# A second level of block multiplication for one of the seven products of gate/up

## The chip, the core and the metric

The kernel runs on one core of a Trainium2 chip. Five engines work side by side, each through its own list of instructions in order: PE (TensorE, matmuls; its weight loads are shown as PEld), DVE (VectorE, elementwise work on two tensors), ACT (ScalarE, activations and copies), POOL (GpSimd) and SP (SyncE, which here only issues DMAs). An engine that must wait for another waits at the instruction that needs it, and everything behind that instruction on the same engine waits as well. The metric is the time of one execution on the device in microseconds; lower is better.

## The reference

Two layers of an encoder trunk of width 1024 over 1040 tokens. Each layer has a mixer and then a SwiGLU feed-forward network with 2816 hidden units. The change lies in the feed-forward network alone:

```python
def swiglu(h, w_gate_up, w_down):
    gate, up = jnp.split(h @ w_gate_up.astype(h.dtype), 2, axis=-1)
    return (jax.nn.silu(gate) * up) @ w_down.astype(h.dtype)

for l in range(DEPTH):
    h = h + hybrid_mixer(rmsnorm(h, norm1_w[l]), ...)
    h = h + swiglu(rmsnorm(h, norm2_w[l]), w_gate_up[l], w_down[l])
```

Everything is float32. [...]

## The kernel before

**Gate/up.** The hidden units are cut into 22 tiles of 128 (FT = 22). For one tile f the weights are a 2 x 2 block matrix: A11 and A12 are the gate's weights for the first and the second half of the model width, A21 and A22 the up's; each block is 512 x 128, held as 4 pieces of 128 x 128. The tokens' x is a 2 x 2 block matrix too: model width by token half, each half 520 tokens in layer 0 (the 16 meta tokens included) and 512 in layer 1. The eight block products are made as seven, by Strassen's scheme in Winograd's form: A11·B11, A12·B21, S1·T1, S2·T2, S3·T3, S4·B22 and A22·T4, where S1 to S4 are sums of weight blocks and T1 to T4 sums of x blocks. The T's are made once a layer, the S's for each tile.

Of one tile, four DMAs on SP load the blocks; A21, A22 and the two sums' tiles come from a ring of five buffers (`ck2`). DVE makes the sums (lines 1373 to 1378). `w_op` splits a block: ACT writes the high part (line 1089), DVE the low part (line 1090); the pairs go round seven slots. `prod` issues a product's matmuls, three for each of the 4 k pieces (lines 1108 to 1110). In layer 0 a half of 520 columns does not go into one bank of PSUM, so each product runs as two groups of 260 columns (NJ = 2); in layer 1 it is one group of 512. Products that share a bank are added up by PE; DVE adds or ACT copies each out to `g` and `u` (lines 1391 to 1422). The seventh, p4, adds A22·T4 to the bank that holds S2·T2 + S3·T3 and the sum goes to u's first half:

```python
            def p4(j):
                prod(ps["b", j], W["A22"], T["T4"], j, False)
                tt(out=part(u, 0, j), in0=pin(ps["b", j]), in1=part(u, 0, j), op=ALU.add)
```

Behind the products DVE and ACT form silu(g·r)·u·r on whole rows of 1040 or 1024 columns (lines 1436 to 1439), a DMA stores the row to `ad`, and for the first 11 tiles DVE also writes a difference of its halves to `td`. The first four tiles (NE = 4) have A11·B11 and A12·B21 done ahead, under the end of the mixer, so five products are left there.

**Down.** The product with w_down follows the same seven-product scheme, in units of 3 x 128 hidden units by 128 outputs. Its sums of weights (S1, S2, S3, each in place of the last) are made by `s_sum`; `a_load` loads the 192 KB blocks for them. The first S1 sums are made inside gate/up by `s_under`: in the code, sum n stands behind tile n + 8, for n from 0 to 7 (S_UP = 8), with one buffer U of tag `c` (two buffers) for both loads. The rest are made under the units of down's first product.

**What sets the order.** The code is written product by product; a scheduler then orders each engine's list by priority (the order of the code) and by the times of its own model, with buffers taken when they are free. So an instruction stands in an engine's list where the scheduler found it ready, not where the code has it: the first S sums, written behind tile 8 and later, stand in DVE's list among the first tiles. The chip runs each list strictly in order.

Of the kernel before, what the change touches and what calls it, by code (L numbers as in the profile page):

```python
# [42 lines left out]
def trunk(ctx: ExitStack, tc: tile.TileContext, xT, w_in, w_ba, w_out, w_gu, w_dn,  # L43
# [267 lines left out]
    for l in range(DEPTH):  # L311
# [900 lines left out]
        S_UP = 8  # L1212
# [35 lines left out]
        def s_sum(which, n, room=None):  # L1248

            S = s_raw(n)  # L1250
            if which == "S1":
                r, o = room or (s_room(), s_room())
                tt(out=S, in0=a_load(r, 1, 0, n), in1=a_load(o, 1, 1, n), op=ALU.add)
            elif which == "S2":
                tt(out=S, in0=S, in1=a_load(s_room(), 0, 0, n), op=ALU.subtract)
            else:
                tt(out=S, in0=a_load(s_room(), 1, 1, n), in1=S, op=ALU.subtract)

        def s_under(f):

            n = f - 8
            if 0 <= n < S_UP:
                s_raw(n)
                if n == 0:
                    s_raw(6)
                    dw["U"] = c4k("U")
                s_sum("S1", n, (dw["U"][:, 0:384], dw["U"][:, 384:768]))
# [76 lines left out]
        def down_begins(p):  # L1344
# [10 lines left out]
            elif p is p1_[2]:  # L1355
                dw["T", 1] = flat("P1", F32R)
                w_unit(3)
                w_unit(4)
                t_pair(3)
        for f in range(FT):  # L1360
            A11, A12, A21, A22 = raw4("raw"), raw4("raw"), raw4("ck2"), raw4("ck2")
# [17 lines left out]
            for n, a in ([("S3", A21), ("A22", A22), ("S4", s2t)] if end else  # L1379
                         [("S4", s2t), ("S3", A21), ("A12", A12), ("A22", A22)]):  # L1380
                if f >= NE or n != "A12":
                    W[n] = w_op(a)
            g, u = early[f] if f < NE else (row((X[1], Y[1])[f % 2] + "f"), row(X[1], F32, 3))
# [27 lines left out]
            def p7(j):  # L1411
                prod(ps["b", j], W["S3"], T["T3"], j, False)
                tt(out=part(u, 1, j), in0=pin(ps["b", j]), in1=part(u, 1, j), op=ALU.add)

# [16 lines left out]
            else:  # L1431
                for j in range(NJ):
                    for p in (p1, p5, p3, p6, p7, p2, p4):
                        p(j)
            gv, uv, rv = g[:, o0:L], u[:, o0:L], ss[:, o0:L]
            tt(out=gv, in0=gv, in1=rv, op=ALU.mult)
            tt(out=uv, in0=uv, in1=rv, op=ALU.mult)
            act(out=gv, in_=gv, func=AF.Silu)
            tt(out=uv, in0=uv, in1=gv, op=ALU.mult)
            dma(ad[f][:, o0:L], uv)  # L1440
            if f < NP:
                tt(out=gv[:, 0:NB].rearrange("p (g e) -> p g e", g=2), in0=half(uv, 1), in1=half(uv, 0), op=ALU.subtract)
                dma(td[f], gv[:, 0:NB])
            s_under(f)


# [227 lines left out]
```

## Time and profile before

| | us |
|---|---|
| median of 3 runs | 2451.37 |
| lowest and highest run | 2449.09 and 2451.5 |
| the profiled execution | 2449.55 |
| its span, first to last instruction | 2447.5 |
| gate/up of layer 0, end of tile 4 to end of tile 20 | 684.5 to 1002.2 |
| gate/up of layer 1, end of tile 4 to end of tile 20 | 1893.0 to 2197.6 |

Ends of tiles are the ends of line 1436's multiplications. In rows of engines or windows, a number of us is the time in which the engine was busy, x the count of instructions. In rows of the timeline the first number is the start in us, the second the duration, and a bracket holds the idle time before and what ended it. Names of tiles are the buffers' tags: `a`, `b`, `a3`, `b3f` and so on are reused through the layers, `rw` is tag ck2, `whi` and `wlo` are weight slots, `pa`, `pb`, `pf`, `pacc` the PSUM banks. In rows with a bare name the number is left out.

### The profile page before, as it was taken

How to read it: one execution, taken by the hardware profiler on the slowest of the kernel's cores; microseconds unless marked ns; L12 is line 12 of the kernel's file. 1: busy time of each engine (PE TensorE's matmuls, PEld its weight loads, DVE VectorE, ACT ScalarE, POOL GpSimd, SP SyncE). 2: the span in 40 equal slices, each digit the busy share in tenths (PEclk: the TensorE clock that was granted, in tenths of full speed). 3: DMA queues.
4: the chain of work that ended last, by engine and by line, in shares of the span. 5: the costliest groups of instructions: out<-in, count | busy, mean ns of one | idle time of the engine just before them, and what ended most of it. 6: DMA issues, size and time to landing. Idle time of an engine off the chain costs nothing. (4 is left out here: it accounts for less than half of the span.)

```text
span 2447.5 us, 44866 instructions
## 1 busy us (share of the span) xinstructions
PE 2427.6 (99%) x17366; PEld 2234.8 (91%) x17366; DVE 1794.2 (73%) x3313; ACT 1026.3 (42%) x1918; POOL 183.6 (8%) x285
## 2 busy tenths in 40 slices
PE   9999999999999999999999999999999999999998
PEld 8989999999999999999999988998988888888887
DVE  6789355869877777797856883557798777768886
ACT  5744322435333333444546543224453333334464
POOL 0360000011000000000001400010110000000000
PEclk9999999999999999999999999999999999999999
DMA  3436165623432222665524551556334222228733
GB/s 134 164 112 145 66 213 159 216 86 105 158 119 95 84 79 79 213 219 166 161 80 145 156 126 62 176 170 228 121 115 153 99 95 82 83 96 274 234 103 129
DMA packets 256509, 336.32 MB, mean 137 GB/s; under 512 B 92021, under 2 KB 148793, under 8 KB 256297
## 3 DMA queue, kind: packets, MB, share of 16 engines
q1 hardware_dynamic: 208024, 299.37, 38.1%
q0 software_dynamic: 8448, 21.42, 2.8%
q10 hardware_dynamic: 39824, 12.68, 2.1%
q8 instruction: 136, 2.23, 0.4%
q14 instruction: 77, 0.62, 0.1%
HBM read 254.52 MB, written 78.86 MB: 136 GB/s over the span
## 5 line engine op out<-in xcount | busy, mean ns | idle before, releaser
L177 PE MATMUL pacc<-a,whi 128*128 128x346 f32 (+1 forms) x752 | 244.4, 328 | 4.0 <-DVE b L329 2.3
L179 PE MATMUL pacc<-a,wlo 128*128 128x346 f32 (+1 forms) x752 | 242.9, 325 | 0.1
L177 PE MATMUL pacc<-b,whi 128*128 128x342 f32 (+3 forms) x648 | 225.7, 349 | 0.0
L179 PE MATMUL pacc<-b,wlo 128*128 128x342 f32 (+3 forms) x648 | 223.4, 347 | 0.0
L178 PE MATMUL pacc<-a,whi 128*128 128x346 f32 (+1 forms) x646 | 211.2, 327 | 0.0
L178 PE MATMUL pacc<-b,whi 128*128 128x342 f32 (+3 forms) x559 | 192.8, 345 | 0.0
L132 ACT ACTIVATE whi<-raw 128x512 fp32r<-128x512 f32 x144 | 89.8, 628 | 243.6 <-PE pacc L178 177.4
L177 PEld LDWEIGHTS pacc<-a,whi 128*128 128x128 f32 x752 | 141.3, 189 | 9.9 <-issue 4.1
L133 DVE TENSOR_TENSOR wlo<-raw,whi 128x512 fp32r<-128x512 f32 x144 | 106.0, 739 | 56.0 <-ACT whi L132 55.0
L179 PEld LDWEIGHTS pacc<-a,wlo 128*128 128x128 f32 x752 | 141.8, 189 | 1.7 <-issue 0.8
L179 PEld LDWEIGHTS pacc<-b,wlo 128*128 128x128 f32 x648 | 122.4, 189 | 10.4 <-issue 1.7
L177 PEld LDWEIGHTS pacc<-b,whi 128*128 128x128 f32 x648 | 122.4, 189 | 8.5 <-issue 0.6
L178 PEld LDWEIGHTS pacc<-a,whi 128*128 128x128 f32 x646 | 122.1, 189 | 3.8 <-issue 2.3
L1089 ACT ACTIVATE whi<-rw 128x512 fp32r<-128x512 f32 x98 | 61.4, 631 | 137.7 <-DVE rw L1377 43.9
L178 PEld LDWEIGHTS pacc<-b,whi 128*128 128x128 f32 x559 | 105.8, 189 | 7.8 <-issue 1.3
L1089 ACT ACTIVATE b<-rw 128x512 fp32r<-128x512 f32 x65 | 40.6, 631 | 132.9 <-PE pacc L1109 39.6
L1089 ACT ACTIVATE a<-rw 128x512 fp32r<-128x512 f32 x65 | 40.8, 630 | 112.7 <-PE pacc L1109 78.5
L1090 DVE TENSOR_TENSOR wlo<-rw,whi 128x512 fp32r<-128x512 f32 x98 | 67.3, 688 | 5.6 <-ACT whi L1089 4.9
L329 DVE TENSOR_TENSOR b<-pacc,rstd 128x346 f32<-128x346 f32 (+1 forms) x63 | 32.3, 512 | 34.7 <-PE pacc L179 34.3
L1326 DVE TENSOR_TENSOR P<-b,P 128x520 fp32r<-128x520 f32 (+1 forms) x71 | 48.3, 695 | 10.4 <-ACT P L1325 10.3
L1544 PE MATMUL pacc<-P,a 128*128 128x260 f32 x196 | 55.4, 283 | 0.0
L1542 PE MATMUL pacc<-P,a 128*128 128x260 f32 x196 | 55.3, 282 | 0.0
(1043 smaller groups left out, 8011.9 us busy)
## 6 DMA issues: line engine op xcount, KB each, us to landing
raw<-in_w_in SPq DMA_DIRECT2D x112, 256.0 KB, 2.8
rw<-in_w_gu SPq DMA_DIRECT2D x96, 256.0 KB, 2.7
raw<-in_w_gu SPq DMA_DIRECT2D x96, 256.0 KB, 2.8
rec<-vkd SPq DMA_DIRECT2D x61, 256.0 KB, 2.9
b<-ad SPq DMA_DIRECT2D x55, 260.0 KB, 3.6
a<-ad SPq DMA_DIRECT2D x55, 256.0 KB, 3.8
rw<-in_w_dn SPq DMA_DIRECT2D x68, 192.0 KB, 3.6
ad<-a SPq DMA_DIRECT2D x21, 520.0 KB, 2.9
```

The lines of the kernel that those rows point to most:

```text
L132: lastw[0] = act(out=hi, in_=raw[:, 0:kk, :], func=AF.Copy)
L133: lastw[1] = tt(out=lo, in0=raw[:, 0:kk, :], in1=hi.bitcast(F32), op=ALU.subtract)
L177: mm(ps[:, :n], wh, xh[:, n0:n1], start=(k == 0), stop=False)
L178: mm(ps[:, :n], wh, xl[:, n0:n1], start=False, stop=False)
L179: mm(ps[:, :n], wl, xh[:, n0:n1], start=False, stop=(k == K - 1))
L329: tt(out=t[:, n0:n1], in0=ps, in1=rstd[:, n0:n1], op=ALU.mult)
L1089: act(out=hi, in_=src, func=AF.Copy)
L1090: tt(out=lo, in0=src, in1=hi.bitcast(F32), op=ALU.subtract)
L1326: tt(out=lo, in0=r, in1=hi.bitcast(F32), op=ALU.subtract)
L1542: mm(ps, wh[:, k, :], th[:, c0:c1], start=st and k == 0, stop=False, skip_group_check=True)
L1544: r = mm(ps, wl[:, k, :], th[:, c0:c1], start=False, stop=e, skip_group_check=True)
```

## The change

Tiles 4 to 19 go in eight pairs (f even, f odd). For a pair the product A22·T4 is itself a 2 x 2 block product: rows are the two tiles' A22, the inner dimension is cut in two halves of two k pieces, and the columns of T4 into two parts (260 or 256). `second_level` makes it by the same scheme with seven sub-products of two k pieces each, in three banks (pA, pC, pD); pA gets four of them one after the other and is added out to `u` after each. It loads both A22 once more, makes four sums of half blocks, and splits three and a half blocks (`wa`, `ws`, `wt`, `wz`) in place of two. S3·T3 is now added to both halves of u, since p4 no longer follows in its bank. u stays unfinished until the pair is done; every third g of these tiles moves to a buffer of tag `c`.

The x sums that the sub-products need are made once a layer by `quarters`, in four parts written behind tiles 1, 2, 3 and 4, into three rows that the first tiles' g leave and one buffer of tag `c`.

S_UP goes from 8 to 4, and `s_under` loads these four sums' blocks behind tile 19 and adds them behind tile 20.

On DVE, in the first tiles of layer 0: ahead, before the change, a piece from the end of tile 0's work; L1253 are S1 sums of down (`b_820` is the sum, `U` the loaded block), L1437 to L1442 finish a tile, L1090 are low parts of weights, L1406 and L1409 add products to g.

```order
L1442 TENSOR_TENSOR b_613_6137<-a_614_6138 128x520
L1374 TENSOR_TENSOR rw_6958<-rw_6957,raw_6949 128x512
L1422 TENSOR_TENSOR a_624_6211<-pf_6637,a_624_6211 128x260
L1253 TENSOR_TENSOR b_820_8275<-U_8277 128x384
L1406 TENSOR_TENSOR b_623_6210<-pb_6704,a_624_6211 128x260
L1090 TENSOR_TENSOR wlo_6803<-rw_6781,whi_6802 128x512
L1409 TENSOR_TENSOR b_623_6210<-pacc_6705,b_623_6210 128x260
L1406 TENSOR_TENSOR b_633_6283<-pb_6807,a_634_6284 128x260
L1436 TENSOR_TENSOR b_623_6210<-b_623_6210,rstd_5487 128x1040
L1409 TENSOR_TENSOR b_633_6283<-pa_6808,b_633_6283 128x260
L1406 TENSOR_TENSOR b_633_6283<-pf_6875,a_634_6284 128x260
L1253 TENSOR_TENSOR b_820_8275<-U_8277 128x384
```

After it, a piece that stands earlier on DVE, among the weights of tiles 0 and 1; L1378 to L1380 are the first x sums (`tr` their buffer, `a_649` is T4), L1452, L1453 and L1457 weight sums.

```order
L1090 TENSOR_TENSOR wlo_6455<-rw_6442,whi_6454 128x512
L1378 TENSOR_TENSOR tr_6778<-a_649_6417 128x520
L1379 TENSOR_TENSOR tr_6778<-a_649_6417 128x520
L1457 TENSOR_TENSOR rw_6609<-raw_6607,rw_6609 128x512
L1090 TENSOR_TENSOR wlo_6461<-rw_6436,whi_6460 128x512
L1453 TENSOR_TENSOR rw_6616<-rw_6615,raw_6607 128x512
L1090 TENSOR_TENSOR a_661_6449<-rw_6615,a_661_6449 128x512
L1380 TENSOR_TENSOR tr_6778<-tr_6778 128x520
L1489 TENSOR_TENSOR b_613_6137<-pacc_6465,a_614_6138 128x260
```

The S sums have left the first tiles, and the x sums stand there, the first of them before tile 0's first addition to g (L1489).

On DVE, in the middle of layer 0's gate/up: before, the end of one tile's second half. L1413 adds S3·T3 to u's second half and L1422 A22·T4 to its first, L1437 and L1439 finish u (`a_918`), the other rows belong to the next tiles.

```order
L1413 TENSOR_TENSOR a_918_9250<-pacc_9347,a_918_9250 128x260
L1090 TENSOR_TENSOR a_661_6449<-rw_9449,a_661_6449 128x512
L1395 TENSOR_TENSOR a_938_9482<-pb_9484,a_938_9482 128x260
L1374 TENSOR_TENSOR rw_9688<-rw_9687,raw_9679 128x512
L1422 TENSOR_TENSOR a_918_9250<-pacc_9347,a_918_9250 128x260
L1437 TENSOR_TENSOR a_918_9250<-a_918_9250,rstd_5487 128x1040
```

After, the end of a pair: L1420 are the additions from the second level's banks to the two u (`a_932`, `a_952`), L1496 and L1498 the two additions of S3·T3.

```order
L1420 TENSOR_TENSOR a_932_9100<-pf_9487,a_932_9100 128x260
L1090 TENSOR_TENSOR wlo_9564<-rw_9554,whi_9563 128x512
L1521 TENSOR_TENSOR b3f_9299<-b3f_9299,rstd_5487 128x1040
L1420 TENSOR_TENSOR a_932_9100<-pb_9489,a_932_9100 128x260
L1456 TENSOR_TENSOR rw_9554<-raw_9546,rw_9554 128x512
L1496 TENSOR_TENSOR a_952_9300<-pacc_9385,a_952_9300 128x260
L1498 TENSOR_TENSOR a_952_9300<-pacc_9385,a_952_9300 128x260
L1090 TENSOR_TENSOR a_661_6449<-rw_9554,a_661_6449 128x512
L1420 TENSOR_TENSOR a_932_9100<-pf_9487,a_932_9100 128x260
L1420 TENSOR_TENSOR a_952_9300<-pacc_9488,a_952_9300 128x260
```

One addition behind each tile's last product has become seven behind each pair, mixed with the next tile's weights and sums; bank pA is pf_9487 here.

The diff:

```diff
         td = dram.tile([NP, 128, NB], F32, name=nm("td"))
         dw = {}
         nr = [0, 0, 0]
-        S_UP = 8
+        S_UP = 4
 
         def flat(tag, dt=F32):
             return big(tag, dt).rearrange("p a b -> p (a b)")
...
                 return dw["X"][:, 384 * r:384 * r + 384]
             return dw["B"][:, 5 * NB + 384 * (r - 2):5 * NB + 384 * (r - 2) + 384]
 
-        def s_sum(which, n, room=None):
+        def s_sum(which, n):
 
             S = s_raw(n)
             if which == "S1":
-                r, o = room or (s_room(), s_room())
-                tt(out=S, in0=a_load(r, 1, 0, n), in1=a_load(o, 1, 1, n), op=ALU.add)
+                tt(out=S, in0=a_load(s_room(), 1, 0, n), in1=a_load(s_room(), 1, 1, n), op=ALU.add)
             elif which == "S2":
                 tt(out=S, in0=S, in1=a_load(s_room(), 0, 0, n), op=ALU.subtract)
             else:
...
 
         def s_under(f):
 
-            n = f - 8
-            if 0 <= n < S_UP:
-                s_raw(n)
-                if n == 0:
-                    s_raw(6)
-                    dw["U"] = c4k("U")
-                s_sum("S1", n, (dw["U"][:, 0:384], dw["U"][:, 384:768]))
+            for n in range(S_UP):
+                if f == FT - 3:
+                    if n % 2 == 0:
+                        dw["U", n // 2] = c4k("U")
+                    a_load(s_raw(n), 1, 0, n)
+                    dw["u", n] = a_load(dw["U", n // 2][:, 384 * (n % 2):384 * (n % 2) + 384], 1, 1, n)
+                elif f == FT - 2:
+                    tt(out=s_raw(n), in0=s_raw(n), in1=dw["u", n], op=ALU.add)
 
         def w_unit(u):
 
...
                 w_unit(3)
                 w_unit(4)
                 t_pair(3)
+        tq = {}
+
+        def quarters(n):
+
+            v = lambda t, k0, j: t[:, k0:k0 + 2, E * j:E * j + E].bitcast(F32)
+            hi, lo = T["T4"]
+            if n == 0:
+                two_rows = c4k("tr")
+                tq["raw"] = [two_rows[:, NB * q:NB * q + NB].rearrange("p (k e) -> p k e", k=2) for q in range(2)]
+            a, b = tq["raw"]
+
+            def split(i, r):
+                t = row(Y[1], F32R, 3) if i != 3 else sb.tile([128, L], F32R, tag="c", bufs=2, name=nm("tq"))
+                tq[i] = [t[:, NB * q:NB * q + NB].rearrange("p (k e) -> p k e", k=2) for q in range(2)]
+                act(out=tq[i][0], in_=r, func=AF.Copy)
+                tt(out=tq[i][1], in0=r, in1=tq[i][0].bitcast(F32), op=ALU.subtract)
+
+            if n == 0:
+                tt(out=a, in0=v(hi, 0, 1), in1=v(hi, 0, 0), op=ALU.subtract)
+                tt(out=b, in0=v(lo, 0, 1), in1=v(lo, 0, 0), op=ALU.subtract)
+                tt(out=a, in0=a, in1=b, op=ALU.add)
+                split(1, a)
+            elif n == 1:
+                tt(out=b, in0=v(hi, 2, 1), in1=a, op=ALU.subtract)
+                tt(out=b, in0=b, in1=v(lo, 2, 1), op=ALU.add)
+                split(2, b)
+            elif n == 2:
+                tt(out=a, in0=v(hi, 2, 0), in1=b, op=ALU.subtract)
+                tt(out=a, in0=a, in1=v(lo, 2, 0), op=ALU.add)
+                split(4, a)
+            else:
+                tt(out=b, in0=v(hi, 2, 1), in1=v(hi, 0, 1), op=ALU.subtract)
+                tt(out=a, in0=v(lo, 2, 1), in1=v(lo, 0, 1), op=ALU.subtract)
+                tt(out=b, in0=b, in1=a, op=ALU.add)
+                split(3, b)
+
+        def second_level(f, us):
+
+            Rf, Rg = raw4("ck2"), raw4("ck2")
+            dma(Rf, w_gu[l, f - 1, 1, :, 4:8, :])
+            dma(Rg, w_gu[l, f, 1, :, 4:8, :])
+            SA, SB = raw4("ck2"), raw4("ck2")
+            a, b = slice(0, 2), slice(2, 4)
+            tt(out=SA[:, a], in0=Rg[:, a], in1=Rg[:, b], op=ALU.add)
+            tt(out=SA[:, b], in0=SA[:, a], in1=Rf[:, a], op=ALU.subtract)
+            tt(out=SB[:, a], in0=Rf[:, a], in1=Rg[:, a], op=ALU.subtract)
+            tt(out=SB[:, b], in0=Rf[:, b], in1=SA[:, b], op=ALU.subtract)
+            wa, ws, wt, wz = w_op(Rf), w_op(SA), w_op(SB), w_op(Rg[:, b])
+            pick = lambda w, q: [t[:, q] for t in w]
+            bx = lambda k0, j: [t[:, k0:k0 + 2, E * j:E * j + E] for t in T["T4"]]
+            pA, pC, pD = pbank(), pbank(), pbank()
+
+            def sub(ps, w, t, first):
+                for k in range(2):
+                    mm(ps[:, :E], w[0][:, k, :], t[0][:, k, :], start=first and k == 0, stop=False, skip_group_check=True)
+                    mm(ps[:, :E], w[0][:, k, :], t[1][:, k, :], start=False, stop=False, skip_group_check=True)
+                    mm(ps[:, :E], w[1][:, k, :], t[0][:, k, :], start=False, stop=k == 1, skip_group_check=True)
+
+            def to(i, j, ps):
+                v = half(us[i][:, o0:L], 0)[:, j, :]
+                tt(out=v, in0=ps[:, :E], in1=v, op=ALU.add)
+
+            sub(pA, pick(wa, a), bx(0, 0), True)
+            to(0, 0, pA)
+            sub(pC, pick(ws, a), tq[1], True)
+            to(1, 1, pC)
+            sub(pD, pick(wa, b), bx(2, 0), True)
+            to(0, 0, pD)
+            sub(pA, pick(ws, b), tq[2], False)
+            to(0, 1, pA)
+            sub(pC, pick(wt, b), bx(2, 1), False)
+            to(0, 1, pC)
+            sub(pA, pick(wt, a), tq[3], False)
+            to(1, 1, pA)
+            sub(pA, wz, tq[4], False)
+            to(1, 0, pA)
+
+        waiting = []
         for f in range(FT):
+            two = NE <= f < FT - 2
             A11, A12, A21, A22 = raw4("raw"), raw4("raw"), raw4("ck2"), raw4("ck2")
             dma(A11, w_gu[l, f, 0, :, 0:4, :])
             dma(A21, w_gu[l, f, 1, :, 0:4, :])
...
             tt(out=A21, in0=A11, in1=A21, op=ALU.subtract)
             for n, a in ([("S3", A21), ("A22", A22), ("S4", s2t)] if end else
                          [("S4", s2t), ("S3", A21), ("A12", A12), ("A22", A22)]):
-                if f >= NE or n != "A12":
+                if (f >= NE or n != "A12") and not (two and n == "A22"):
                     W[n] = w_op(a)
-            g, u = early[f] if f < NE else (row((X[1], Y[1])[f % 2] + "f"), row(X[1], F32, 3))
+            if f < NE:
+                g, u = early[f]
+            else:
+                g = c4k("g") if two and f % 3 == 2 else row((X[1], Y[1])[(f % 3 if two else f) % 2] + "f")
+                u = row(X[1], F32, 3)
             ps = {}
 
 
...
             def p7(j):
                 prod(ps["b", j], W["S3"], T["T3"], j, False)
                 tt(out=part(u, 1, j), in0=pin(ps["b", j]), in1=part(u, 1, j), op=ALU.add)
+                if two:
+                    tt(out=part(u, 0, j), in0=pin(ps["b", j]), in1=part(u, 0, j), op=ALU.add)
 
             def p2(j):
                 if f >= NE:
...
                     down_begins(p)
             else:
                 for j in range(NJ):
-                    for p in (p1, p5, p3, p6, p7, p2, p4):
+                    for p in (p1, p5, p3, p6, p7, p2, p4)[:6 if two else 7]:
                         p(j)
-            gv, uv, rv = g[:, o0:L], u[:, o0:L], ss[:, o0:L]
+            gv, rv = g[:, o0:L], ss[:, o0:L]
             tt(out=gv, in0=gv, in1=rv, op=ALU.mult)
-            tt(out=uv, in0=uv, in1=rv, op=ALU.mult)
+            if not two:
+                tt(out=u[:, o0:L], in0=u[:, o0:L], in1=rv, op=ALU.mult)
             act(out=gv, in_=gv, func=AF.Silu)
-            tt(out=uv, in0=uv, in1=gv, op=ALU.mult)
-            dma(ad[f][:, o0:L], uv)
-            if f < NP:
-                tt(out=gv[:, 0:NB].rearrange("p (g e) -> p g e", g=2), in0=half(uv, 1), in1=half(uv, 0), op=ALU.subtract)
-                dma(td[f], gv[:, 0:NB])
+            waiting.append((f, g, u))
+            if f == NE:
+                quarters(3)
+            if two and f % 2 == 0:
+                continue
+            if two:
+                second_level(f, [w[2] for w in waiting])
+            for (n, g, u) in waiting:
+                gv, uv = g[:, o0:L], u[:, o0:L]
+                if two:
+                    tt(out=uv, in0=uv, in1=rv, op=ALU.mult)
+                tt(out=uv, in0=uv, in1=gv, op=ALU.mult)
+                dma(ad[n][:, o0:L], uv)
+                if n < NP:
+                    tt(out=gv[:, 0:NB].rearrange("p (g e) -> p g e", g=2), in0=half(uv, 1), in1=half(uv, 0), op=ALU.subtract)
+                    dma(td[n], gv[:, 0:NB])
+            waiting.clear()
             s_under(f)
+            if 0 < f < NE:
+                quarters(f - 1)
 
 
         hb = [big(X[0][0]), big(X[0][1])]
```

## The prediction

> **What bounds the kernel now.** I read the page's busy shares and chain first, then the windows by stage, then the waits and the timeline of the places that the change touches.
>
> ```profile
> PE 2427.6 (99%) x17366; PEld 2234.8 (91%) x17366; DVE 1794.2 (73%) x3313; ACT 1026.3 (42%) x1918; POOL 183.6 (8%) x285
> PE 40%; DVE 2%; DMA 1%; issue 1%; ACT 1%; ACTq 0%; SPq 0%; DVEq 0%; POOLq 0%
> ```
>
> PE is busy for 99% of 2447.5 us and alone carries the chain that ended last; fewer or shorter matmuls are the only thing that shortens the kernel, and any new wait of PE lengthens it. The profiled execution took 2449.55 us; the median of the three runs, 2451.37, is 1.8 above it.
>
> The windows by stage: gate/up of layer 0 (its first three tiles, then the tiles from 4 on), of layer 1 (the same two), and two pieces of layer 0's down stage.
>
> ```profile
> core 0: us, PE busy (x) PEld busy (x) DVE busy (x) ACT busy (x) POOL busy (x), PEclk, DMA share, GB/s
> 593.00:666.00 73.00, 71.47 (x590) 69.94 (x589) 65.47 (x111) 27.12 (x44) 0.00 (x0) 1.00 0.42 140
> 684.00:1008.00 324.00, 324.00 (x2705) 324.00 (x2705) 236.90 (x393) 108.80 (x196) 0.00 (x0) 1.00 0.26 88
> 1815.00:1863.00 48.00, 48.00 (x208) 38.53 (x206) 43.40 (x67) 18.18 (x27) 0.00 (x0) 1.00 0.44 140
> 1890.00:2198.00 308.00, 308.00 (x1333) 249.79 (x1332) 222.90 (x316) 100.64 (x159) 0.00 (x0) 1.00 0.27 92
> 1012.00:1048.00 36.00, 36.00 (x302) 36.00 (x301) 26.46 (x49) 16.21 (x31) 0.00 (x0) 1.00 1.03 360
> 1050.00:1090.00 40.00, 40.00 (x336) 40.00 (x336) 38.89 (x85) 18.57 (x37) 0.00 (x0) 1.00 0.67 206
> ```
>
> In the long part of gate/up PE never pauses and DVE has room (236.90 of 324 is 73%, 222.90 of 308 is 72%). In the first tiles DVE is at 90% in both layers (65.47 of 73, 43.40 of 48), and only in layer 0 does PE pause there, for 1.53 us. In the down stage the DMA engines are full for 36 us and then DVE is at 97%, yet PE does not wait.
>
> **What a matmul costs.** PE's records overlap, so the price is the distance of starts. First and last of 31 matmuls of 260 columns (layer 0), of 18 of 512 (layer 1), of 57 of 256 (the last stage):
>
> ```profile
> 800.29 0.28 PE L1108 MATMUL pacc<-P,a 128*128 128x260 f32 x1
> 803.90 0.28 PE L1108 MATMUL pf<-P,a 128*128 128x260 f32 x1
> ...
> 2100.03 0.39 PE L1108 MATMUL pb<-a,whi 128*128 128x512 f32 x1
> 2103.97 0.40 PE L1109 MATMUL pacc<-P,b 128*128 128x512 f32 x1
> ...
> 2421.79 0.28 PE L1544 MATMUL pacc<-P,wlo 128*128 128x256 f32 x1
> 2428.30 0.27 PE L1543 MATMUL pf<-P,b 128*128 128x256 f32 x1
> ```
>
> 3.61/30 = 0.1203 us, 3.94/17 = 0.2318 us, 6.51/56 = 0.1163 us.
>
> **The product A22·T4 (saved).** For a pair of tiles it was, in layer 0, 2 tiles x 2 halves x 4 k x 3 = 48 matmuls of 260 columns; now 7 sub-products x 2 k x 3 = 42. That is 6 x 0.1203 = 0.72 us a pair, 5.8 us over 8 pairs. In layer 1 it was 24 matmuls of 512 columns, 5.56 us; now 42 of 256, 4.88 us: 0.68 a pair, 5.4 us in all. Together 11.2 us, the whole of the gain.
>
> The layer-1 term rests on halving the columns halving the price. A weight load per matmul does not shrink: PEld is full in layer 0 (324.00 of 324) and 81% in layer 1 (249.79 of 308). The row of 256 columns settles it, 0.1163 against half of 0.2318, 0.1159. [...]
>
> **DVE per pair (added).** Starts of consecutive DVE instructions give its prices:
>
> ```profile
> 608.36 0.69 DVE L1090 TENSOR_TENSOR wlo<-rw,whi 128x512 fp32r<-128x512 f32 x1
> 608.96 0.69 DVE L1378 TENSOR_TENSOR rw<-raw,rw 128x512 f32<-128x512 f32 x1
> ...
> 650.05 0.42 DVE L1422 TENSOR_TENSOR a<-pa,a 128x260 f32<-128x260 f32 x1
> 650.39 0.42 DVE L1422 TENSOR_TENSOR a<-pacc,a 128x260 f32<-128x260 f32 x1
> ...
> 652.81 1.24 DVE L1437 TENSOR_TENSOR a<-a,rstd 128x1040 f32<-128x1040 f32 x1
> 653.96 0.70 DVE L1442 TENSOR_TENSOR b<-a 128x520 f32<-128x520 f32 x1
> 654.57 1.24 DVE L1439 TENSOR_TENSOR a<-a,b 128x1040 f32<-128x1040 f32 x1
> ```
>
> 0.60 us for 512 columns, 0.61 for 520, 0.34 for 260 (taken for 256 too), 1.15 for 1040. Per pair go two weight splits (1.2). Come three and a half splits (2.1 + one of 256 columns, 0.34), four weight sums of 256 columns (1.36) and seven additions out of the banks (2.38); the second addition behind S3·T3 replaces the one behind A22·T4. Net +5.0 us a pair. A pair's DVE time before is 0.73 x 40.4 = 29.5 us in layer 0 (2 x 168 matmuls x 0.1203 is 40.4) and 28.2 of 38.9 in layer 1; after, 34.5 of 39.7 and 33.2 of 38.3: 87%, between the 73% at which PE did not pause and the 90% at which it paused 1.53/73 = 2.1%. ACT gains 1.5 activations of about 0.6 us on a third of its time: nothing. Two more loads of 256 KB a pair go on DMA engines at 26%: nothing of themselves, but A21, A22 and four more tiles now pass through the same five buffers, 12 a pair instead of 8, so weights are ready later, and behind a load that waits on SP stand the next tile's loads.
>
> Bounds for PE's new waits over the 634 us behind the first tiles: 0, by the long windows, and 2.1% or 13.3 us, by the first tiles of layer 0. Layer 1's first tiles had no pause at 90%, so I stay near the lower end: 0.5% in layer 0 (1.7 us), 0.2% in layer 1 (0.6): 2.3 us.
>
> **The x sums in four parts (added); the S sums (moved).** 10 additions and 4 splits of 520 columns (512 in layer 1) at 0.61 us are 8.5 us of DVE a layer, in its fullest stretch. What leaves that stretch is large as well: the eight sums of down weights, written behind tiles 8 to 15, run in the first tiles, and DVE, which works in order, stands before them until their loads land.
>
> ```profile
> 617.46 0.69 DVE L1373 TENSOR_TENSOR rw<-rw,rw 128x512 f32<-128x512 f32 x1 [1.36 <-DMA rw<-in_w_gu]
> 635.10 0.56 DVE L1253 TENSOR_TENSOR b<-U 128x384 f32<-128x384 f32 x1 [1.37 <-DMA td<-b]
> 639.57 0.56 DVE L1253 TENSOR_TENSOR b<-U 128x384 f32<-128x384 f32 x1 [0.47 <-DMA U<-in_w_dn]
> 640.05 0.68 DVE L1090 TENSOR_TENSOR a<-rw,a 128x512 fp32r<-128x512 f32 x1
> ...
> L1253 DVE TENSOR_TENSOR b<-U x6: 547/555/559, 635.1 to 670.6; 128x384 f32<-128x384 f32 x6
>   DMA U<-in_w_dn: 5.2, 4
>   DMA td<-a: 1.8, 1
>   DMA td<-b: 1.4, 1
> ...
> PE pacc L1108 <- ACT whi L1089: 1.2, 2, 0.7
> PE pacc L1108 <- DVE b L1409: 0.2, 1, 0.2
> ...
> rw<-in_w_dn SPq DMA_DIRECT2D x68, 192.0 KB, 3.6
> ```
>
> Eight sums at 0.48 us (639.57 to 640.05) are 3.8 us a layer, and the 8.4 us of waiting in both layers is 4.2 each: 8.0 us leave, 8.5 come, so the stretch as a whole is no fuller. The places differ: the order sets the first five x additions, 3.0 us, among the splits for the first two tiles (from 609 us on), 20 us ahead of where the sums stood, and there PE already waits for splits and sums (the two rows of PE). The 1.36 us that DVE waits for a load at 617 takes part of it. So PE loses 3.0 − 1.4 = 1.6 us in layer 0. Layer 1 has the same five and no pause of PE there: I take 1.0. Bounds a layer: a gain of the 0.2 us at 641 that the first sums' wait precedes, and 8.5 us if all the new work came ahead of PE. Term: 2.6 us.
>
> **The S sums at their new places.** Four are loaded behind tile 19 into rows that the x parts held until tile 19's last sub-product; on SP, A22 and A12 of tile 21 stand behind two of these loads, with tile 20's products (168 x 0.1203 = 20 us) as cover: 0. If that cover is gone, it costs one load's landing, 3.6 us by the last row above, in each layer. The other four are summed in the down stage: 4 x 2 x 192 KB = 1.6 MB more at 360 GB/s is 4.4 us of DMA where the engines are full (1.03), and 1.9 us of DVE shortly before its 97%. The order puts most of these loads behind the first product's x loads, and PE had no wait at 97%, so I take 0.5 us a layer of a possible 0 to 4.4: 1.0 us.
>
> **The sum.** 11.2 − 2.3 − 2.6 − 1.0 = 5.3 us gained. Against the profiled execution 2444.3, against the median 2446.1; I say 2445.0, 0.26% under the median. What a measurement here can tell from no change is about 0.2%, 4.9 us, so the limits are 2446.5 and 2456.3.
>
> **Rivals.**
>
> *DVE delays PE a little in every pair, and the gain is gone.* Layer 0 at the first tiles' 2.1% over its 324 us pays 6.8 us instead of 1.7, layer 1 1.5 instead of 0.6: 6.0 less, net −0.7, 2450 to 2452, say 2451. For it: 87% is nearer to 90 than to 73, and weights that share five buffers come later. Against: DVE's room is spread over a pair of 39.7 us.
>
> *The bank of four sub-products becomes the bound: slower.* In second_level one bank, pA, gets four sub-products; after each, DVE must have added it out before the next one may write there, three times a pair. If DVE is in one of its 1.15 us instructions each time that counts once in a pair, PE stands 1.15 us a pair, 18.4 us over 16 pairs in place of 2.3: 2449.55 − 11.2 + 18.4 + 3.6 = 2460.4. It decides from (11.2 − 3.6)/16 = 0.48 us a pair on. For it: three sub-products are only 0.7 us long, less than one long DVE instruction. Against: in the pair of layer 0 whose additions are shown ahead, the order sets 28 to 36 other matmuls, 3.4 us and more, between two writes of pA.
>
> *A fixed price per matmul.* If 42 short ones with their weight loads cost more than 24 long ones (over 5.56/42 = 0.132 us each), layer 1 turns round; at 0.150 it loses 0.74 a pair, and the sum is 5.8 − 5.9 − 5.9 = −6.0: 2455.6. The 256-column rows stand against it; it keeps 0.03. [...]
>
> **How the numbers follow.** Forecast (faster) 0.50; gain eaten, within 0.2%, 0.27; bank pA 0.20; fixed price 0.03, near the upper limit, counted with slower. So faster 0.50, same 0.27, slower 0.23. The range runs from 2439.5 (all new waits near their lower ends: 2449.55 − 11.2 = 2438.4, a little above it) to 2457 (the second rival at 0.94 us a pair); above lies a little over 0.1, below under 0.1.
>
> **What the profile after would show.** PE: 96 matmuls more (48 fewer of 260 columns, 144 more that stand for halves of 512), 42 of them in lines of second_level per pair, their starts 0.12 apart; a pair of tiles from 4 on in 39.7 us in layer 0 and 38.3 in layer 1. DVE near 87% there. PE's waits in the first tiles of layer 0 grow from 1.5 to about 3 us, on splits of weights. No wait of DVE on loads of U in the first tiles. The forecast is wrong if PE's waits for DVE or ACT in gate/up behind the first tiles pass 3 us, if the pairs are longer than 39.9 and 38.5, or if the down stage begins with PE waiting for x or weights.

## The result and the profile after

The changed kernel takes 2458.12 us in the median (2455.67 to 2461.12), the kernel before 2450.32 beside it: a ratio of 1.0032, 95% interval 1.0024 to 1.0040. It is slower by 0.3%; the forecast was 2445.0, the range 2439.5 to 2457.0. The profiled execution of the changed kernel took 2461.12 us, its span 2459.1, so it is 3.0 above its median. Of the 11.6 us between the two spans 3.5 arose in the mixers (1.66 ahead of layer 0's gate/up, 1.82 between layer 0's down and layer 1's gate/up), which the change does not touch; the rest is in gate/up and down.

The page's busy shares and the engines' shares of the chain that ended last:

```profile
PE 2423.4 (99%) x17462; PEld 2236.4 (91%) x17462; DVE 1874.8 (76%) x3549; ACT 1047.2 (43%) x1958; POOL 184.3 (7%) x285
PE 38%; DVE 4%; DMA 2%; issue 1%; ACT 1%; SPq 0%; ACTq 0%; POOL 0%; DVEq 0%; POOLq 0%
```

PE has the 96 matmuls more that were forecast and is busy for 4.2 us less, yet the span is longer: the time is in PE's pauses. In the chain DVE has gone from 2% to 4%, DMA from 1% to 2%.

The same windows by stage as before, moved to where the stages now lie (first tiles and long part of layer 0, of layer 1, then the piece of layer 0's down stage in which DVE had been at 97%):

```profile
594.65:667.65 73.00, 69.98 (x572) 67.99 (x571) 67.85 (x116) 27.15 (x44) 0.00 (x0) 1.00 0.35 116
690.00:1012.00 322.00, 322.00 (x2688) 322.00 (x2687) 268.36 (x500) 117.94 (x216) 0.00 (x0) 1.00 0.32 105
1823.20:1871.20 48.00, 47.14 (x203) 37.54 (x202) 46.54 (x71) 18.27 (x28) 0.00 (x0) 1.00 0.35 111
1900.00:2208.00 308.00, 307.51 (x1490) 256.01 (x1489) 257.40 (x418) 109.23 (x177) 0.00 (x0) 1.00 0.32 106
1050.00:1090.00 40.00, 39.51 (x330) 39.29 (x329) 33.90 (x70) 18.69 (x37) 0.00 (x0) 1.00 0.71 219
```

In the long parts PE still does not pause, with DVE at 83% and 84%. The last row is the odd one: DVE, which had 38.89 us of work in these 40, now has 33.90, and it is not that there is less to do.

PE's longest pauses, from its timeline (start, duration, and in brackets the idle time before and what ended it):

```profile
614.39 0.39 PE L1110 MATMUL pacc<-b,a 128*128 128x260 f32 x1 [0.73 <-DVE a L1090]
616.88 0.39 PE L1110 MATMUL pf<-P,a 128*128 128x260 f32 x1 [0.54 <-DVE a L1090]
...
683.98 0.39 PE L1108 MATMUL pacc<-b,a 128*128 128x260 f32 x1 [1.59 <-DVE a L1478]
687.88 0.39 PE L1108 MATMUL pf<-P,whi 128*128 128x260 f32 x1 [2.20 <-ACT b3f L1503]
...
1091.76 0.36 PE L1642 MATMUL pf<-P,whi 128*128 128x260 f32 x1 [2.25 <-DVE a L1667]
...
2290.86 0.77 PE L1642 MATMUL pb<-P,whi 128*128 128x512 f32 x1 [3.65 <-DVE b L1667]
```

None of these was there before. Since PE's records overlap (a matmul of 260 columns is shown for 0.28 us, and the next starts 0.12 us behind it), the time lost is larger by the overlap: by the distance of starts the last four cost 1.76, 2.36, 2.41 and 3.81 us.

**Where the time went.** Lengths of stages from PE's starts; a stage ends with the first matmul of the next. "Down, P5" is down's second product, "down, rest" begins with the first matmul of its third, P3.

| us | before | after | difference |
|---|---|---|---|
| layer 0: first four tiles | 60.17 | 62.30 | +2.13 |
| tile 4 to the end of down's first product | 394.17 | 392.78 | −1.39 |
| down, P5 | 31.61 | 34.03 | +2.42 |
| down, rest | 157.97 | 159.54 | +1.57 |
| layer 1: first four tiles | 55.91 | 56.99 | +1.08 |
| tile 4 to the end of down's first product | 380.63 | 377.67 | −2.96 |
| down, P5 | 30.63 | 34.42 | +3.79 |
| down, rest | 155.64 | 157.11 | +1.47 |
| sum | 1266.73 | 1274.84 | +8.11 |

The 8.1 us agree with the 7.8 us between the medians. 9.25 us of loss are in down, whose own matmuls the change does not touch.

**The stop in down.** P3 goes on in the banks of P5, so its first matmul must wait until DVE has added P5's sums out of them (L1667). DVE's waits for loads between 1000 and 1092 us, and rows of its timeline (L1252 are S1 sums, L1254 S2 sums):

```profile
DVE b L1252 <- DMA b3f<-in_w_dn: 2.6, 3, 1.2
DVE b L1252 <- DMA b<-in_w_dn: 1.4, 2, 0.9
...
DVE b L1254 <- DMA b<-in_w_dn: 1.1, 1, 1.1
...
DVE b L1254 <- DMA b3f<-in_w_dn: 0.6, 1, 0.6
DVE S L1252 <- DMA b3f<-in_w_dn: 0.5, 1, 0.5
```

```profile
1070.57 0.42 DVE L1252 TENSOR_TENSOR b<-b3f,b 128x256 f32<-128x256 f32 x1 [0.90 <-DMA b<-in_w_dn]
...
1072.48 0.43 DVE L1252 TENSOR_TENSOR b<-b,b3f 128x256 f32<-128x256 f32 x1 [1.15 <-DMA b3f<-in_w_dn]
1073.53 0.56 DVE L1254 TENSOR_TENSOR b<-b,b3f 128x384 f32<-128x384 f32 x1 [0.62 <-DMA b3f<-in_w_dn]
...
1077.01 0.56 DVE L1254 TENSOR_TENSOR b<-b,b 128x384 f32<-128x384 f32 x1 [1.14 <-DMA b<-in_w_dn]
...
1091.18 0.43 DVE L1667 TENSOR_TENSOR a<-pf,a 128x260 f32<-128x260 f32 x1
```

DVE stands for 6.2 us before sums whose blocks have not landed; the same view of the kernel before lists no wait for a load there in layer 0. Its waits for other things are no longer than before, 12.1 us against 15.0. In layer 1 the waits for loads are 5.7 us, against 1.6 before. The rooms into which the blocks go (two in row `b3f`, two in `b`) are few, and the next load into one starts only when DVE has used the last: between 1000 and 1092 us SP, which issues these loads, waits 10.4 us for L1252 and L1254. From 1077 on DVE is busy without a gap (14.17 of 14.18 us) and never catches up: the addition that PE waits for stands at 1091.18 behind some 14 us of other work.

**The stop at tile 4.** ACT's row, then DVE's:

```profile
687.45 0.39 ACT L1503 ACTIVATE b3f<-pf 128x260 f32<-128x260 f32 x1 [2.96 <-DMA td<-b3f]
```

```profile
679.86 1.24 DVE L1536 TENSOR_TENSOR c<-c,b3f 128x1040 f32<-128x1040 f32 x1
...
682.88 0.70 DVE L1539 TENSOR_TENSOR b3f<-c 128x520 f32<-128x520 f32 x1
683.50 0.42 DVE L1478 TENSOR_TENSOR a<-pacc,a 128x260 f32<-128x260 f32 x1
...
687.45 0.43 DVE L1489 TENSOR_TENSOR b3f<-pacc,a 128x260 f32<-128x260 f32 x1 [2.22 <-DMA td<-b3f]
```

Tile 3's g has always been in `b3f`. The diff's new rule for g's row, f % 3 in place of f % 2, gives tile 4 this same row; before, it took the other one. Tile 3 must be finished and its difference stored from `b3f` to `td` before tile 4's first copy may be written there. DVE's last work on tile 3 (L1536, L1539) therefore stands ahead of an addition that frees a bank (L1478, first pause), and ACT and DVE then both wait for the store (second pause).

### The profile page after: what moved, and what is told of

Its sections match the earlier page's. It is cut to its first block, busy times and chain, and to the rows that moved or that the text cites. A ratio compares the mean times of both kernels' runs of the same rounds, so it can differ in the third digit from the quotient of the medians.

```text
span 2459.1 us, 45475 instructions
## 1 busy us (share of the span) xinstructions
PE 2423.4 (99%) x17462; PEld 2236.4 (91%) x17462; DVE 1874.8 (76%) x3549; ACT 1047.2 (43%) x1958; POOL 184.3 (7%) x285
## 5 line engine op out<-in xcount | busy, mean ns | idle before, releaser
L179 PEld LDWEIGHTS pacc<-b,wlo 128*128 128x128 f32 x648 | 122.8, 190 | 10.4 <-issue 1.7
L1089 ACT ACTIVATE whi<-rw 128x512 fp32r<-128x512 f32 (+1 forms) x120 | 73.4, 615 | 136.8 <-PE pf L1109 30.6
L1090 DVE TENSOR_TENSOR wlo<-rw,whi 128x512 fp32r<-128x512 f32 (+1 forms) x120 | 80.2, 670 | 5.4 <-ACT whi L1089 4.7
L1089 ACT ACTIVATE b<-rw 128x512 fp32r<-128x512 f32 (+1 forms) x70 | 42.7, 616 | 72.4 <-PE pacc L1109 26.6
L1089 ACT ACTIVATE a<-rw 128x512 fp32r<-128x512 f32 (+1 forms) x70 | 42.6, 616 | 61.1 <-PE pacc L1109 16.2
L1326 DVE TENSOR_TENSOR P<-a,P 128x512 fp32r<-128x512 f32 (+1 forms) x71 | 48.0, 692 | 11.3 <-ACT P L1325 11.3
L1644 PE MATMUL pacc<-P,a 128*128 128x260 f32 x196 | 55.4, 283 | 0.0
```

The lines of the kernel that those rows point to most:

```text
L179: mm(ps[:, :n], wl, xh[:, n0:n1], start=False, stop=(k == K - 1))
L1089: act(out=hi, in_=src, func=AF.Copy)
L1090: tt(out=lo, in0=src, in1=hi.bitcast(F32), op=ALU.subtract)
L1326: tt(out=lo, in0=r, in1=hi.bitcast(F32), op=ALU.subtract)
L1644: r = mm(ps, wl[:, k, :], th[:, c0:c1], start=False, stop=e, skip_group_check=True)
```

## Experiments

All times are medians; the ratios are to the kernel before, run beside each, with 95% intervals. Line numbers are each kernel's own. The expectations speak of a stop "behind down's first product": by the products' order in the trace it stands at the start of the third. The intervals of experiments 2, 3 and 7 include 1: by their times these kernels cannot be told from the kernel before, and what they show is read against the changed kernel and from the stages.

**1. The S sums alone.** The kernel before with one number changed.

```diff
-        S_UP = 8
+        S_UP = 4
```

> The kernel before with S_UP = 4 and nothing else: sums 4 to 7 of down weights are left to the down stage, as in the changed kernel, without the second level and the x sums in parts. Theory (the four extra sums in down are what stops PE behind down's first product): PE waits 2 to 4 us for DVE's additions at the start of the second product in each layer, runs 1.6 us at a lower clock behind that, and the time is 2450.3 + 2.4 + 3.8 + 2 x 1.6 = about 2459.7 (2456 to 2461). Rival (the stop comes from the second level, which brings tile 21 and its rows later): no wait there, 2449 to 2452.

Measured: 2461.12 us, 1.0047 (1.0032 to 1.0062). PE's rows:

```profile
1091.08 0.36 PE L1542 MATMUL pf<-P,whi 128*128 128x260 f32 x1 [1.71 <-DVE a L1567]
...
2290.53 0.76 PE L1542 MATMUL pb<-P,whi 128*128 128x512 f32 x1 [4.22 <-DVE b L1567]
```

The stop needs no second level. Four sums left to down make the kernel before as slow as the changed one, and the time is 0.1 above the range that was expected. P5 grows by 1.88 and 4.36 us, the rest by 0.10 and 1.50, together 7.8; another 1.3 us are lost in gate/up. PE's waits in layer 0's first tiles grow from 1.4 to 1.8 us, so there the S sums' leaving by itself gave nothing.

**2. Other rows for g.** The three buffers in another turn.

```diff
-                g = c4k("g") if two and f % 3 == 2 else row((X[1], Y[1])[(f % 3 if two else f) % 2] + "f")
+                g = c4k("g") if two and f % 3 == 0 else row((X[1], Y[1])[(f % 3 - 1 if two else f + 1) % 2] + "f")
```

> The changed kernel with g's three buffers taken in another turn, so that tile 4 takes the row that stands free and not the one that tile 3 has just left. Theory (the 4.1 us of PE at tiles 4 and 5 of layer 0, 0.8 in layer 1, come from ACT and DVE waiting for tile 3's rows to be stored): these waits go, 2458.1 - 4.9 = 2453.2. Rival (DVE at 87% is late there, whatever rows are used): the waits stay, 2457 to 2459. The last g also leaves the row in which down's weight sums are loaded one tile earlier: if that matters, another 1 to 3 us.

Measured: 2447.24 us, 0.9992 (0.9982 to 1.0001): 10.9 less than the changed kernel, more than expected. On DVE, tile 4's first additions to g now stand early, in row `a3f`, without a wait for a store; in layer 1 PE still stops in down:

```profile
672.29 0.43 DVE L1489 TENSOR_TENSOR a3f<-pacc,a 128x260 f32<-128x260 f32 x1 [0.68 <-PE pacc L1110]
...
683.39 0.42 DVE L1489 TENSOR_TENSOR a3f<-pf,a 128x260 f32<-128x260 f32 x1
...
2278.42 0.47 PE L1642 MATMUL pb<-P,whi 128*128 128x512 f32 x1 [3.15 <-DVE b L1667]
```

Layer 0 from tile 4 to the end of down's first product takes 388.55 us, 4.23 less than in the changed kernel, and PE has no pause there. The stop in layer 0's down has gone as well. The edit does two things, since the last tile's g also leaves the row in which S blocks are loaded; experiment 8 parts them.

**3. All eight S sums early again.** In the changed kernel, behind tiles 19 and 20.

```diff
-        S_UP = 4
+        S_UP = 8
...
-            for n in range(S_UP):
-                if f == FT - 3:
-                    if n % 2 == 0:
-                        dw["U", n // 2] = c4k("U")
-                    a_load(s_raw(n), 1, 0, n)
-                    dw["u", n] = a_load(dw["U", n // 2][:, 384 * (n % 2):384 * (n % 2) + 384], 1, 1, n)
-                elif f == FT - 2:
-                    tt(out=s_raw(n), in0=s_raw(n), in1=dw["u", n], op=ALU.add)
+            if f == FT - 3:
+                for n in range(S_UP):
+                    a_load(s_raw(n), 1, 0, n)
+                U = c4k("U")
+                for n in range(2):
+                    dw["u", n] = a_load(U[:, 384 * n:384 * n + 384], 1, 1, n)
+            elif f == FT - 2:
+                for n in range(S_UP):
+                    o = dw["u", n] if n < 2 else a_load(raw4("ck2").rearrange("p a b -> p (a b)"), 1, 1, n)
+                    tt(out=s_raw(n), in0=s_raw(n), in1=o, op=ALU.add)
```

> The changed kernel with all eight early sums of down weights made behind tiles 19 and 20 again (four more than it makes there). Theory: the stop behind down's first product goes, with the lower clock behind it: 2458.1 - 9.4 = 2448.7, if tiles 20 and 21 take the eight loads and four sums without waiting. Rival (the stop has another cause): 2457 to 2459, with PE still waiting 2 to 4 us at the start of the second product.

Measured: 2448.19 us, 0.9993 (0.9984 to 1.0003). P5 and the rest of down are back at the lengths before in both layers (31.61 and 157.98, 30.62 and 155.64). Tiles 20 and 21 take the loads and sums without a pause of PE. The pauses at tile 4 of layer 0 stay, 1.76 and 2.03 us.

**4. Both edits.**

> Both edits of the two kernels ahead in one. Theory (two separate losses, which add): 2458.1 - 4.9 - 9.4 = 2443.8, faster than before by 6.5 us, which is the saved matmuls less the first tiles' waits. Rival (the second level's work on DVE finds another place to be late, so that a removed wait comes back elsewhere): 2448 or more.

Measured: 2443.49 us, 0.9977 (0.9967 to 0.9986). The gains do not add: 10.9 and 9.9 would make 20.8, it is 14.6, because experiment 2 alone had already won back 3.8 us in layer 0's down and 1.9 in layer 1's, which experiment 3 wins back as well: 5.7 of the 6.2. The stages sum to 643.92 − 3.46 = 640.46 in layer 0 and 622.81 − 2.55 = 620.26 in layer 1: 6.0 us below the kernel before, where the theory said 6.5.

**5. The x sums tied to later places.** In the kernel of both edits.

```diff
-        def quarters(n):
+        def quarters(n, prev=None):
...
-                tt(out=a, in0=v(hi, 0, 1), in1=v(hi, 0, 0), op=ALU.subtract)
+                after(tt(out=a, in0=v(hi, 0, 1), in1=v(hi, 0, 0), op=ALU.subtract), prev)
...
-            tt(out=gv, in0=gv, in1=rv, op=ALU.mult)
+            g_done = tt(out=gv, in0=gv, in1=rv, op=ALU.mult)
...
-                quarters(f - 1)
+                quarters(f - 1, g_done)
```

(and `after` in the same way around the first instruction of each further part.)

> The kernel of both edits (2443.5), with the x sums in parts tied behind the finished g of tiles 1, 2 and 3, so that the first of them no longer stands among the weights of tiles 0 and 1. Theory (PE's new waits in the first tiles, 2.1 us in layer 0 and 1.1 in layer 1, come from the places of these sums on DVE, not from their number): the waits of 0.9 and 0.7 us near the start of layer 0's first tiles and of 0.7 us in layer 1 go, 2441 to 2442. Rival (DVE is full in the first tiles, so the same time is lost later in them): 2443 to 2445, with PE waiting at tiles 2 to 5.

Measured: 2441.18 us, 0.9961 (0.9946 to 0.9976), the fastest of all. The first tiles of layer 0 in the kernel of both edits, then in this one (same window, counted from the stage's start):

```profile
594.40:667.40 73.00, 69.92 (x571) 67.92 (x570) 67.79 (x115) 27.09 (x44) 0.00 (x0) 1.00 0.35 115
```

```profile
594.11:667.11 73.00, 71.20 (x588) 69.61 (x586) 66.46 (x113) 26.96 (x44) 0.00 (x0) 1.00 0.37 117
```

PE's pauses are down to 1.80 us (before the change 1.53), and the stage takes the 60.17 us that it took before; layer 1's takes 55.80. The work on DVE is nearly the same (91% of the window against 93%), so it was the places. In layer 1 the first tiles gain 0.77 us and the stretch behind them loses 1.19 (378.67 against 377.48). The intervals of experiments 4 and 5 overlap; the stage shows the difference, not the medians.

**6. The second level in layer 0 alone.** In the kernel of both edits, with the turn of g's rows in layer 1 as before the change.

```diff
-            two = NE <= f < FT - 2
+            two = l == 0 and NE <= f < FT - 2
...
-            if f == NE:
+            if l == 0 and f == NE:
                 quarters(3)
...
-            if 0 < f < NE:
+            if l == 0 and 0 < f < NE:
                 quarters(f - 1)
```

> The kernel of both edits (2443.5), with the second level and the x sums in parts in layer 0 alone; layer 1 keeps its product A22 times T4 of 512 columns. It measures what 42 matmuls of 256 columns save against 24 of 512. Theory (118.1 ns against 231.9 in the trace: 0.6 us a pair, 4.8 in all, less 0.8 to 1.1 in the first tiles): 2443.5 + 3.8 = about 2447.3. Rival (the shorter matmuls and their DVE work give layer 1 nothing): 2443 to 2444.

Measured: 2446.64 us, 0.9983 (0.9974 to 0.9993). Layer 1's stages sum to 622.73, the length before the change (622.81), against 620.26 with the second level: it is worth 2.5 us in layer 1 (3.15 by the medians, whose intervals overlap), less than the 3.8 expected.

**7. Fewer loads in down, the same additions.** In the changed kernel, for sums 4 to 7.

```diff
-                tt(out=S, in0=a_load(s_room(), 1, 0, n), in1=a_load(s_room(), 1, 1, n), op=ALU.add)
+                one = S if n < 8 else a_load(s_room(), 1, 0, n)
+                tt(out=S, in0=one, in1=a_load(s_room(), 1, 1, n), op=ALU.add)
...
                     tt(out=s_raw(n), in0=s_raw(n), in1=dw["u", n], op=ALU.add)
+            for n in {FT - 3: (4, 5), FT - 2: (6, 7)}.get(f, ()):
+                a_load(s_raw(n), 1, 0, n)
```

> The changed kernel, in which sums 4 to 7 of down weights are still added in down, but one operand of each is loaded behind tiles 19 and 20 straight into the sum's place, so that down loads four blocks fewer and its four rooms are used less. DVE's four additions stay. Theory (late loads, for which DVE stands in order, stop PE behind down's first product): the 2.4 us and the lower clock of layer 0 go and at least half of layer 1's 5.4 us: 2458.1 - 4.0 - 2.7 = 2451.4 or less. Rival (the 1.9 us of additions themselves make DVE late): 2456 to 2458.

Measured: 2450.38 us, 0.9997 (0.9987 to 1.0007). PE's rows:

```profile
1090.12 0.36 PE L1645 MATMUL pf<-P,whi 128*128 128x260 f32 x1 [0.60 <-DVE a L1670]
...
2282.82 0.47 PE L1645 MATMUL pb<-P,whi 128*128 128x512 f32 x1 [1.12 <-DVE b L1670]
```

With four blocks fewer through the rooms and all the additions left, the stops fall from 2.41 to 0.77 and from 3.81 to 1.28 us, and nothing is lost behind them. DVE's waits for loads in layer 0 fall from 6.2 to 4.1 us. So in the changed kernel it is mostly the late loads, for which DVE stands in order. Their sum alone does not give the length of the stop: in layer 0 experiment 1 has 3.1 us of them and a stop of 1.88, experiment 2 has 3.5 and no stop. It must count when they fall, which no run isolated. The remainder may be the additions or the loads that are left; that was not parted.

**8. Tile 4's row alone.** As experiment 2 up to tile 18, the last rows as in the changed kernel.

```diff
-                g = c4k("g") if two and f % 3 == 2 else row((X[1], Y[1])[(f % 3 if two else f) % 2] + "f")
+                g = c4k("g") if two and f % 3 == 0 else row((X[1], Y[1])[(f % 3 - 1 if two and f < FT - 3 else f) % 2] + "f")
```

> The changed kernel with g's three buffers in the turn of the second experiment up to tile 18, so that tile 4 takes the free row, but the last three tiles keep the rows that they have in the changed kernel, so that the row for down's weight sums comes free with the last tile as there. It parts the two things that the second experiment (2447.2) did at once. Theory (two causes: tile 4's row, 4.9 us, and the late row for the sums' loads, which stops PE in layer 0's down): 2458.1 - 4.9 = 2453.2, no wait of PE at tiles 4 and 5, and still a stop of 2 us or more behind down's first product of layer 0. Rival (the stop in down went because tile 4's did): 2447 to 2449, without a stop there in layer 0.

Measured: 2455.03 us, 1.0012 (1.0002 to 1.0022). PE's row in layer 0's down, and DVE's longest waits for loads there:

```profile
1086.03 0.56 PE L1642 MATMUL pf<-P,whi 128*128 128x260 f32 x1 [3.11 <-DVE a L1667]
```

```profile
DVE b L1252 <- DMA b3f<-in_w_dn: 3.4, 2, 2.7
DVE b L1252 <- DMA b<-in_w_dn: 2.3, 2, 1.3
```

Tiles 4 and 5 are free of pauses (388.64 us, 4.14 less than in the changed kernel; layer 1 1.05 less), but the stop in down is there, and longer: 3.27 us in layer 0 in place of 2.41, 5.23 in layer 1 in place of 3.81. Of the 5.2 us gained in gate/up, 3.2 are given back in down (the stages P5 and rest: +0.78 and +2.38): PE arrives earlier there and the blocks do not (DVE's waits for loads in layer 0 are 8.1 us in place of 6.2). That is also why experiment 2, in which the row for the blocks came free a tile earlier, gained more than tile 4's pauses. In layer 1 experiment 2 still has a stop of 3.31 us; why the earlier row helps less there stays open.

## Why the prediction was wrong

- **The product A22·T4, 11.2 us, less 2.3 for PE's new waits: held.** 8.9 were forecast for the stretch behind the first tiles. In the kernel of both edits, where nothing else disturbs it, it is 5.61 in layer 0 (394.17 − 388.56) and 3.15 in layer 1 (380.63 − 377.48), 8.8 together. That the sum fits so well is luck, since the split is wrong: 4.1 and 4.8 were forecast, and layer 0's 1.5 too few hide layer 1's 1.65 too many. Layer 0 loses 0.2 of its 5.8, not 1.7. In layer 1 the 256-column matmuls start 118.1 ns apart in the mean (318 of them between 1907 and 2208 us), not 116.3, so 24 x 0.2318 − 42 x 0.1181 = 0.60 us a pair and 4.8 in all. Of the 1.65 us that are missing from these 4.8, one wait of PE takes 0.6 in experiment 4, and 512-column matmuls that start 231.9 ns apart in place of 231.5 (some 1150 of them) take 0.5; the rest is open.
- **The first tiles, 2.6 us: held.** 2.13 and 1.08 in the changed kernel, on the splits that were named, and experiment 5 showed the named cause, the x sums' places. That the S sums leave this stretch, which the prediction set against the x sums, gave PE nothing by itself (experiment 1).
- **The S sums at their new places, 1.0 us: the step that failed.** Measured 3.99 in layer 0 (2.42 + 1.57) and 5.26 in layer 1 (3.79 + 1.47): 9.25, and layer 1 beyond the upper bound of 4.4. The bound counted transfer time and DVE time, each against its own cover. What decides is the join of the two: DVE stands in order before a block that comes late through four rooms, and the 97% row of before left it 1.1 us in 40 in which to make up lost time before PE needs P5's sums. "PE had no wait at 97%" was read as slack; it was its end. The price also left out that PE's clock fell to 0.50 for 3.41 us with each stop, of 2.41 and 3.81 us (below). "The order puts most of these loads behind the first product's x loads" looked at the loads and not at who stands behind them.
- **A term that was not there: tile 4's row.** The change of g's rows was described and costed at nothing. It took 4.2 us in layer 0 (392.78 − 388.56) and in layer 1 0.2 (377.67 − 377.48, against the kernel of both edits) to 1.05 (against experiment 8).
- **The rivals.** DVE delaying PE in every pair, and bank pA as the bound, both fell: behind tile 5 of layer 0 the view of PE's waits lists none up to down, and none in layer 1 from 1905 us up to the stop in down. DVE is at 83%, not 87. Of the 5.0 us a pair reckoned for DVE 0.3 are a slip: 2.1 us is already the price of three and a half splits, and the half split's 0.34 was added once more. The price per matmul rose by 1.5%, to 0.118 us, far from the 0.132 us from which the fixed price would decide; its 0.150 us no run shows. That the kernel is slower all the same has another mechanism than any rival gave; two signs of the list did come: PE's waits behind the first tiles pass 3 us (1.59 and 2.20 at tile 4), and "if the down stage begins with PE waiting" nearly names the stop, which is not at its beginning but two products on.

The sum with the measured sizes: −8.8 behind the first tiles, + 4.4 for tile 4's row (4.2 and 0.2), + 3.2 in the first tiles, + 9.25 in down: +8.1 in place of −5.3. With the row and the S sums mended, the mechanism gives 6.0 us by the stages (experiment 4); 11.2 − 2.3 − 2.6 = 6.3 were forecast for it.

## What to carry to other kernels

Cost a moved step by who stands behind it in order on its engine, not by the room that its engine and its transfers have on average: an engine at 97% whose follower does not wait yet has hardly any room (here 1.1 us in 40). What it lost before late loads reached the follower in the changed kernel (in layer 0 6.2 us of waits and a stop of 2.41), in experiment 2 it did not (3.5 us and no stop there). Where a change hands buffers round in another turn, look at the first user after the old scheme: who left that buffer last, and has it been stored? And losses that share one resource need not add (here 10.9 and 9.9 made 14.6 us): one removed early can come back at the next stop, as here 3.2 of 5.2 us.

## What was not expected of the hardware

A stop of PE cost more than its length in some cases and not in others, by what the granted clock did: it fell to 0.50 just behind the stop of 2.41 us in layer 0's down of the changed kernel, where 260-column matmuls then start 0.22 us apart in place of 0.12, and stayed at 1.00 behind one of 3.31 us in experiment 2. Narrow windows place the clock's changes. In the changed kernel it changes at 1092.46, 1095.87, 1454.27, 1461.10, 2290.53 and 2293.95 us: whole multiples of 3.413 us apart (1, 105, 2, 243 and 1). So windows of that trace can be laid on that grid. In the rows below, the number behind the window's length is PE's busy time, and the granted clock is the last column but two. First the window that holds the 2.41 us stop in layer 0's down of the changed kernel and the one behind it; then the two that hold the pauses of 1.76 and 2.36 us at tile 4 of the same execution, and the one behind them:

```profile
1089.04:1092.46 3.42, 1.17 (x10) 0.99 (x10) 3.42 (x9) 1.61 (x3) 0.00 (x0) 1.00 0.70 184
1092.46:1095.87 3.41, 3.41 (x18) 3.41 (x17) 3.41 (x10) 0.00 (x0) 0.00 (x0) 0.50 0.92 278
```

```profile
682.86:686.27 3.41, 1.71 (x12) 1.50 (x12) 1.76 (x4) 0.64 (x1) 0.00 (x0) 1.00 0.85 262
686.27:689.68 3.41, 1.80 (x15) 1.80 (x16) 2.13 (x6) 0.67 (x2) 0.00 (x0) 1.00 0.03 12
689.68:693.10 3.42, 3.42 (x31) 3.42 (x30) 1.99 (x4) 1.07 (x1) 0.00 (x0) 1.00 0.02 5
```

Then the pauses of 1.76 and 2.03 us at tile 4 in experiment 3, and the stop of 3.31 us in layer 1's down in experiment 2, in three windows of the same length, the first two of which share it:

```profile
683.41:686.83 3.42, 1.55 (x13) 1.34 (x12) 1.34 (x3) 0.79 (x3) 0.00 (x0) 1.00 0.48 181
686.83:690.24 3.41, 3.41 (x17) 3.41 (x17) 2.80 (x6) 0.92 (x2) 0.00 (x0) 0.50 0.02 5
```

```profile
2273.70:2277.11 3.41, 1.57 (x7) 0.94 (x5) 3.41 (x9) 2.31 (x4) 0.00 (x0) 1.00 0.73 218
2277.11:2280.53 3.42, 2.11 (x9) 1.78 (x10) 3.42 (x7) 0.00 (x0) 0.00 (x0) 1.00 0.91 282
2280.53:2283.94 3.41, 3.41 (x16) 2.75 (x16) 3.41 (x8) 0.53 (x1) 0.00 (x0) 1.00 0.73 229
```

Length alone does not decide: the clock fell behind a stop of 2.41 us and not behind one of 3.31. What fits the rows is how much of a stop falls into one window; no run moved a stop on purpose to try it. In these rows the clock fell behind the windows in which PE was busy for 1.17 and 1.55 us, and held behind those with 1.57, 1.71, 1.80 and 2.11 us. In the changed kernel's gate/up and down it fell once more, behind the one that holds most of the 3.81 us stop of layer 1:

```profile
2287.12:2290.53 3.41, 0.09 (x1) 0.00 (x0) 3.41 (x8) 1.11 (x3) 0.00 (x0) 1.00 0.86 237
2290.53:2293.95 3.42, 3.10 (x7) 2.48 (x8) 3.42 (x8) 0.00 (x0) 0.00 (x0) 0.50 0.99 339
```

In experiment 1 it fell in layer 1's down (a stop of 4.38 us; 0.56 and 0.59 from 2290 to 2292 and on to 2294 us) and not in layer 0's (1.88 us; 1.00 from 1089 to 1099 us). In experiment 8, behind the 3.27 us in layer 0, matmuls start 0.22 us apart from 1086.38 to 1089.20 us, and the clock's mean from 1050 to 1090 us is 0.96. The ends of matmuls are modelled, so PE's busy times, 1.55 against 1.57 above all, are not exact. Nor do they decide elsewhere: in the mixers the clock also fell behind windows with 3.18 us (before, 1445.99 to 1449.40) and 2.62 us (changed kernel, 1450.85 to 1454.27), and at the very end of the kernel behind 2.19 and 2.09 us. In the changed kernel's down the slow stretch lasts one window in each layer (1092.46 to 1095.87, 2290.53 to 2293.95). The matmuls behind the stops there lose about 1.5 us (1.57 and 1.47, the "rest" rows of the table).
